# A decoder layer's embedding projection moved to the front of one core's weight stream

## The chip, the core and the metric

The kernel runs on one core of a Trainium2 chip. A time is the device time of one execution in microseconds (us); times of a kernel are the median of several executions. A profile is one further execution, recorded by the hardware profiler, with its own time. The engines of the core are TensorE (PE; its weight loads are PEld), VectorE (DVE), ScalarE (ACT), GpSimd (POOL) and SyncE (SP); each works through its own instructions in order, and data is moved by 16 DMA engines, which SP, POOL and ACT give transfers to.

## The reference, cut to what matters

One layer on x (512 x 2048, float32) and a per-layer embedding p (512 x 256):

```python
h = rms_norm(x, norm_g)
proj = h @ w_in                      # 2048 x 10800, split into q, k, v, gates, ...
o_a = nsa_attention(...) * silu(z_a)
o_b = spatial_gating(...) * silu(z_b)
merged = g_a * (o_a @ w_up_a) + g_b * (o_b @ w_up_b)
x = x + merged @ w_out
x = x + sigmoid(x @ w_ple_gate) * (p @ w_ple)      # w_ple: 256 x 2048
return rms_norm(x, final_g)
```

The change is about `p @ w_ple`. It needs only inputs; its result is wanted at the end, in the last gate.

## The kernel before, in words

**Arithmetic.** Every float32 operand is split in two: a high part rounded to the type `fp32r` (ACT, `high`, L96, instruction at L98 or L100) and the rest, the low part (DVE, `low`, L102, at L104 or L106). A product is three matmuls, high by high, high by low, low by high, added up in PSUM.

**The stream of jobs.** A `Job` is one product of an activation with a slice of a weight matrix. The jobs stand in one list (`add_job`, L121), and their weights come in this order through one queue: SP loads half a megabyte at a time into `raw`, three buffers (`load_to`, L134); ACT and DVE split it tile by tile into `hi` (four buffers) and `lo` (three) (`split_to`, L143); a load is issued when DVE has made the last low part of the load three places before it. `gemm` (L170) is a generator that issues the matmuls of the jobs; one step of it (`fill(1)`) is one unit of three 512-column matmuls. "T" jobs give a 128 x 512 tile in one PSUM bank (L190 to L192), "N" jobs four tiles of 128 x 512 or less in four banks (L198 to L200). At a job's end its `evac` function is issued. The rest of the kernel is written by hand around the stream: attention and the rest call `fill(n)` between their own instructions, so the order in which instructions stand in each engine's queue is that in which the program text issues them. `background` holds small pieces of work, of which `gemm` issues one or two (`pops`) for each weight tile.

**PSUM.** Eight banks, two for each of the tags g, s, t and o. `xs` is (g, g, s, s), `ys` is (t, t, o, o).

**The start (L548 to L608).** SP loads `g_row` (`norm_g`), the four 1 MB tiles of x and three weight loads. For each tile of 128 rows ACT sums squares (`stats`) and DVE scales (`scale`). TensorE transposes x in 16 pieces of four 128 x 128 blocks (`turn`), and ACT and DVE split each piece out of PSUM into `act_h` and `act_l` (`turned`). From the sixth piece on, two units of the first job, `kc0`, stand between them.

**Order of the jobs.** kc, vc, k, v, q and za (attention); vn, u, zb (gating); for each of 16 columns of tiles ma, mb, ua, ub (merge); then `pl0`, wo0 to wo3 (output projection), pg0, `pl1`, pg1, `pl2`, pg2, `pl3`, pg3 (the last gate). The four `pl` jobs (L456, L541) are p @ w_ple, 512 columns each, on `ys`; all wo and pg jobs have 16 steps of k, with wo on `xs` and `ys` in turn and pg on `xs`. p is loaded by POOL (L1010), transposed behind job ua8 and split into `ph` and `pl` (L1012 to L1016). `evac_ple` (L469) copies a pl job's banks to an SBUF tile `ple` on ACT, and `ple_add` (L477) multiplies it with the gate that ACT made in `evac_ple_gate` (L484) or `evac_last` (L503). At the end of wo3 the 64 KB a partition of `act_h` and `act_l` come free; the pool `fq` (L1027) then takes `fg` (`final_g`, loaded by POOL), `ple`, `th`, `tl` and `sg`.

Of the kernel before, what the change touches and what calls it, by code (L numbers as in the profile page):

```python
# [12 lines left out]
F32 = mybir.dt.float32  # L13
# [7 lines left out]
P = 128  # L21
S = 512
# [29 lines left out]
def kernel(ctx: ExitStack, tc: tile.TileContext, x, p, norm_g, w_in,  # L52
# [15 lines left out]
    def bank(kind, name):  # L68
        return psum.tile([P, 512], F32, tag=kind, name=name)
# [59 lines left out]
        jobs.append(job)  # L129

    raw, parts = {}, {}
    state = {"loads": 0, "high": 0, "low": 0, "ahead": 0, "pops": 2}

    def load_to(i):  # L134
        while state["loads"] <= min(i, len(loads) - 1):
# [34 lines left out]
    def gemm():  # L170
        si = 0
        for job in jobs:
# [4 lines left out]
            k = 0  # L177
            while k < job.kt - job.tail:
                flush()
                split_to(si + state["ahead"] + (k if job.tail else 0))  # L180
# [140 lines left out]
    def evac_c(which, a):  # L321
# [11 lines left out]
            deferred.append(rest)  # L333
        return f

    for a in range(2):
        add_job(Job(f"kc{a}", "T", w_in, C_KV + 128 * a, 128, KT, h_act, evac_c("k", a)))
    for a in range(2):
# [114 lines left out]
                nc.vector.tensor_tensor(out=sl, in0=sl, in1=ps[t], op=ALU.add)  # L453
        return e

    add_job(Job("pl0", "N", w_ple, 0, 512, 2, lambda k: p_act(k), lambda ps: evac_ple(0)(ps), ys))  # L456
    for cg in range(4):
        add_job(Job(f"wo{cg}", "N", w_out, 512 * cg, 512, KT, merged_act, evac_out(cg), (xs, ys)[cg % 2]))

# [2 lines left out]
            oa["l"][:, k] if k < 8 else ob_l[:, k - 8]  # L462

    f_tiles = {}

    def p_act(k):
        return f_tiles["ph"][:, k], f_tiles["pl"][:, k]

    def evac_ple(cg):  # L469
        def e(ps):  # L470
            t = f_tiles["pool"].tile([P, TT, 512], F32, tag="ple", name="ple")
            for i in range(TT):
                nc.scalar.copy(t[:, i], ps[i])
            f_tiles["ple"] = t
        return e
# [8 lines left out]
    def evac_ple_gate(cg):  # L484
        def e(ps):
            sg = [f_tiles["pool"].tile([P, 512], F32, tag="sg", name="sg", bufs=4) for _ in range(TT)]
            for t in range(TT):
                nc.scalar.activation(sg[t], ps[t], AF.Tanh, scale=0.5)
            ple = f_tiles["ple"]

            def add(t):
                ple_add(cg, t, sg[t], ple)

            def squares(t):
                sl = x2[:, t, 512 * cg:512 * cg + 512]
                nc.scalar.activation(sg[t], sl, AF.Square, accum_out=f_tiles["ss"][:, t, cg:cg + 1])
                nc.gpsimd.tensor_tensor(out=sl, in0=sl, in1=f_tiles["fg"][:, 512 * cg:512 * cg + 512], op=ALU.mult)
            for t in range(TT):
                background.append(lambda t=t: add(t))
                background.append(lambda t=t: squares(t))  # L500
        return e

    def evac_last(ps, t):  # L503
# [6 lines left out]
        if t:  # L510
# [4 lines left out]
        sl = ple_add(3, t, sg, f_tiles["ple"])  # L515
        nc.scalar.activation(sg, sl, AF.Square, accum_out=ss[:, t, 3:4])
        nc.vector.tensor_tensor(out=sl, in0=sl, in1=fg[:, 1536:], op=ALU.mult)
        if t == 0:
# [28 lines left out]

    with tc.tile_pool(name="xin", bufs=4, side="right") as xin:  # L548
        xt = [xin.tile([P, D], F32, tag="xt", name=f"xt{t}") for t in range(TT)]
        g_row = xin.tile([KT, P], F32, name="g_row", bufs=1)  # L550
        g_col = xin.tile([P, KT], F32, name="g_col", bufs=1)
        st = xin.tile([P, TT, 2], F32, name="st", bufs=1)
        nc.sync.dma_start(g_row, norm_g.rearrange("(k p) -> k p", p=P))
        for t in range(TT):
            nc.sync.dma_start(xt[t], x[t * P:t * P + P])
        load_to(2)

        def stats(t):
            sq = xin.tile([P, D], BF16, tag="sq", name="sq", bufs=1)
            nc.scalar.activation(sq, xt[t], AF.Square, accum_out=st[:, t, 0:1])  # L560
            nc.scalar.activation(st[:, t, 1:2], st[:, t, 0:1], AF.Sqrt, bias=eps_t, scale=1.0 / D)

        def scale(t):
            nc.vector.reciprocal(st[:, t, 0:1], st[:, t, 1:2])
            nc.vector.tensor_scalar(out=xt[t], in0=xt[t], scalar1=st[:, t, 0:1], scalar2=None, op0=ALU.mult)

        banks = {}

        def turn(hf, kp):

            b = banks[hf, kp] = bank("st"[len(banks) % 2], "ps_x")
            for j in range(4):
                k, t = 2 * kp + j // 2, 2 * hf + j % 2
                nc.tensor.transpose(b[:, j * P:j * P + P], xt[t][:, k * P:k * P + P], ident)

        def turned(hf, kp):
            sl = slice(2 * hf * P, 2 * hf * P + 2 * P)
            for j in range(2):
                k = 2 * kp + j
                split(act_h[:, k, sl], act_l[:, k, sl], banks[hf, kp][:, 2 * P * j:2 * P * (j + 1)],  # L580
                      g_col[:, k:k + 1], later=True)
            flush()

        b = bank("o", "ps_g")
        nc.tensor.transpose(b[:, :KT], g_row, ident[:KT, :KT])
        nc.vector.tensor_copy(g_col, b[:, :KT])
        for t in range(3):
            stats(t)
            if t < 2:
                scale(t)  # L590
        order = [(0, 0), (0, 1), (0, 2), (0, 3), (1, 0), (1, 1), (0, 4), (1, 2), (0, 5), (1, 3), (0, 6), (1, 4), (0, 7),
                 (1, 5), (1, 6), (1, 7)]
        for o in order[:4]:
            turn(*o)
        for i, o in enumerate(order):
            turned(*o)
            if i == 0:
                stats(3)
                scale(2)
                scale(3)  # L600
            if i + 4 < len(order):
                turn(*order[i + 4])
            if o[0] == 1 and o[1] >= 1:
                fill(2)
            elif o == (1, 0):
                split_to(0)
# [397 lines left out]
    f_tiles["ph"] = fp.tile([P, 2, S], F32R, name="ph")  # L1004
    f_tiles["pl"] = fp.tile([P, 2, S], F32R, name="pl")
    f_tiles["ss"] = fp.tile([P, TT, 4], F32, name="ss")
    with tc.tile_pool(name="sigp", bufs=2) as sigp:
        tmp_pool["p"] = sigp
        p_nat = sigp.tile([P, TT, 256], F32, name="p_nat", bufs=1)
        nc.gpsimd.dma_start(p_nat, p.rearrange("(t p) c -> p t c", p=P))  # L1010
        finish("ua8")
        for j in range(2):  # L1012
            b = bank("o", "ps_p")
            for t in range(TT):
                nc.tensor.transpose(b[:, t * P:t * P + P], p_nat[:, t, j * P:j * P + P], ident)
            split(f_tiles["ph"][:, j], f_tiles["pl"][:, j], b)  # L1016
        finish(f"ub{KT - 1}")
    ple0 = ctx.enter_context(tc.tile_pool(name="ple0", bufs=1))
    f_tiles["pool"] = ple0


    free_banks = {0: "gs", 1: "to", 2: "gs", 3: "to"}
    for cg in range(4):
        finish(f"wo{cg}")
        if cg == 3:
            ph_act.close()
            fq = f_tiles["pool"] = ctx.enter_context(tc.tile_pool(name="fq", bufs=2))  # L1027
            fg = f_tiles["fg"] = fq.tile([P, D], F32, name="fg", bufs=1)
            nc.gpsimd.dma_start(fg, bass.AP(tensor=final_g.tensor, offset=final_g.offset, ap=[[0, P], [1, D]]))
            f_tiles["th"] = fq.tile([P, 8, 512], F32R, name="th", bufs=1)  # L1030
            f_tiles["tl"] = fq.tile([P, 8, 512], F32R, name="tl", bufs=1)
            state["pops"] = 1
# [38 lines left out]
```

## Time and profile before

| | |
|---|---|
| time, median of 3 runs | 1666.81 us (1666.53 to 1667.07) |
| the profiled execution's own time | 1666.61 us |
| its span, first to last instruction | 1664.9 us |
| mean granted clock of TensorE | 0.997 |
| busy: PE, PEld, DVE, ACT, POOL | 98%, 82%, 44%, 37%, 6% |
| matmuls and transposes | 7821 |
| DMA | 159.62 MB, mean 96 GB/s |

In the lines of the profile, L12 is line 12 of the kernel; `out<-in` are the program's names for the tiles; a row of a timeline has the start, the duration, engine, line, operation, tiles, shapes and count, and in brackets how long the engine stood idle before it and what released it. Matmuls are pipelined: a 512-column matmul is shown with 0.39 us, while the next one starts sooner than that. In the chain of waits stands the work that ended last, followed back from the last instruction.

### The profile page before, as it was taken

The page shows a single profiled execution, that of the slowest core. Times are in us where ns is not written, and L with a number is a line of the kernel's source. Part 1 is how long each engine was busy: PE and PEld are TensorE (multiplying, and loading weights), DVE is VectorE, ACT ScalarE, POOL GpSimd, SP SyncE. Part 2 cuts the span into 40 slices and gives each one's busy share as a digit, 9 for nine tenths or more (in the row PEclk, how much of TensorE's full clock was granted, in tenths as well). Part 3 has the DMA queues.
Part 4 walks back from the last instruction along what each step waited for, and adds up shares of the span by engine and source line. Part 5 has one row for each costly group of instructions (what it writes and reads, how often), then busy time and mean ns, then how long its engine had stood idle before and what let it go on. Part 6 is the DMA issues. An engine that isn't in the chain of part 4 may idle for free.

```text
span 1664.9 us, 20578 instructions
## 1 busy us (share of the span) xinstructions
PE 1638.9 (98%) x7821; PEld 1367.3 (82%) x7821; DVE 739.0 (44%) x1492; ACT 619.1 (37%) x1255; POOL 107.8 (6%) x136
## 2 busy tenths in 40 slices
PE   6999999999999999999999999999999999999997
PEld 5779888888888888888888888888888888888886
DVE  5343478888873352443223222322235333333335
ACT  6233366676653322332222222222224222223334
POOL 2000010110210011000000000000000000001100
PEclk9999999999999999999999999999999999999999
DMA  6322421111133333334333333333334422333333
GB/s 201 93 76 76 112 64 39 52 51 51 45 113 109 89 89 92 99 90 113 102 96 94 101 94 97 99 91 101 99 92 159 140 93 89 91 125 89 101 101 127
DMA packets 214625, 159.62 MB, mean 96 GB/s; under 512 B 4848, under 2 KB 190336, under 8 KB 212992
## 3 DMA queue, kind: packets, MB, share of 16 engines
q1 hardware_dynamic: 212976, 151.05, 31.3%
q0 software_dynamic: 1408, 6.92, 1.2%
q8 instruction: 61, 1.00, 0.2%
q14 instruction: 36, 0.29, 0.1%
q10 hardware_dynamic: 144, 0.36, 0.1%
HBM read 154.12 MB, written 4.19 MB: 95 GB/s over the span
## 4 chain that ended last, share of the span: by engine, by line
PE 95%; DVE 3%; ACT 1%; DMA 0%; issue 0%; SPq 0%; DVEq 0%; ACTq 0%
PE ps_wo L200 4%; PE ps_wo L198 4%; PE ps_wo L199 3%; PE ps_mb L190 3%; PE ps_ma L190 3%; PE ps_mb L191 3%; PE ps_ma L191 3%; PE ps_ma L192 3%; PE ps_mb L192 3%; PE ps_pg L198 3%; PE ps_pg L200 3%; PE ps_pg L199 3%; PE ps_za L190 2%; PE ps_za L192 2%; PE ps_t L768 2%; PE ps_za L191 2%
## 5 line engine op out<-in xcount | busy, mean ns | idle before, releaser
L104 DVE TENSOR_TENSOR lo<-raw,hi 128x512 fp32r<-128x512 f32 (+1 forms) x536 | 367.4, 688 | 652.9 <-PE ps_mb L192 129.7
L98 ACT CAST hi<-raw 128x512 fp32r<-128x512 f32 (+1 forms) x536 | 328.6, 615 | 730.9 <-PE ps_wo L200 102.5
L198 PE MATMUL ps_wo<-hi,act_h 128*128 128x512 f32 x256 | 100.9, 394 | 0.0
L200 PE MATMUL ps_wo<-hi,act_l 128*128 128x512 f32 x256 | 99.8, 390 | 0.0
L199 PE MATMUL ps_wo<-lo,act_h 128*128 128x512 f32 x256 | 99.7, 390 | 0.0
L190 PE MATMUL ps_ma<-act_h,hi 128*128 128x512 f32 x256 | 99.6, 389 | 0.0
L191 PE MATMUL ps_ma<-act_l,hi 128*128 128x512 f32 x256 | 99.6, 389 | 0.0
L192 PE MATMUL ps_ma<-act_h,lo 128*128 128x512 f32 x256 | 99.6, 389 | 0.0
L190 PE MATMUL ps_mb<-act_h,hi 128*128 128x512 f32 x256 | 99.6, 389 | 0.0
L191 PE MATMUL ps_mb<-act_l,hi 128*128 128x512 f32 x256 | 99.6, 389 | 0.0
L192 PE MATMUL ps_mb<-act_h,lo 128*128 128x512 f32 x256 | 99.6, 389 | 0.0
L98 ACT CAST pth<-ps_t 128x512 fp32r<-128x512 f32 (+1 forms) x88 | 47.9, 544 | 65.7 <-PE ps_t L768 65.4
L729 ACT ACTIVATE prob<-prob,st 128x512 f32<-128x512 f32 (+3 forms) x128 | 70.7, 555 | 4.0 <-DVE st L720 3.8
L104 DVE TENSOR_TENSOR ptl<-ps_t,pth 128x512 fp32r<-128x512 f32 (+1 forms) x88 | 56.3, 640 | 21.1 <-ACT pth L98 20.3
L720 DVE CUSTOM_DVE_ANT_0 prob<-ps_s,b 128x512 f32<-128x512 f32 (+3 forms) x128 | 56.3, 486 | 10.1 <-PE ps_s L717 9.8
L431 POOL TENSOR_TENSOR m<-sig,sig 128x512 f32<-128x512 f32 x16 | 27.1, 1694 | 493.6 <-DVE sig L429 493.6
L200 PEld LDWEIGHTS ps_wo<-hi,act_l 128*128 128x128 f32 x256 | 48.1, 188 | 10.2
L192 PEld LDWEIGHTS ps_mb<-act_h,lo 128*128 128x128 f32 x256 | 48.1, 188 | 10.0
L192 PEld LDWEIGHTS ps_ma<-act_h,lo 128*128 128x128 f32 x256 | 48.1, 188 | 10.0
L190 PEld LDWEIGHTS ps_ma<-act_h,hi 128*128 128x128 f32 x256 | 48.1, 188 | 10.0
L190 PEld LDWEIGHTS ps_mb<-act_h,hi 128*128 128x128 f32 x256 | 48.1, 188 | 10.0
L191 PEld LDWEIGHTS ps_ma<-act_l,hi 128*128 128x128 f32 x256 | 48.1, 188 | 9.9
(311 smaller groups left out, 3663.8 us busy)
## 6 DMA issues: line engine op xcount, KB each, us to landing
raw<-in_w_in_dram SPq DMA_DIRECT2D x164, 512.0 KB, 3.5
raw<-in_w_out_dram SPq DMA_DIRECT2D x32, 512.0 KB, 3.5
raw<-in_w_ple_gate_dram SPq DMA_DIRECT2D x32, 512.0 KB, 3.5
raw<-in_w_up_a_dram SPq DMA_DIRECT2D x16, 512.0 KB, 3.7
raw<-in_w_up_b_dram SPq DMA_DIRECT2D x16, 512.0 KB, 3.7
xt<-in_x_dram SPq DMA_DIRECT2D x4, 1024.0 KB, 8.0
m<-in_x_dram POOLq DMA_DIRECT2D x4, 1024.0 KB, 8.6
out_dram<-m SPq DMA_DIRECT2D x3, 1024.0 KB, 3.9
```

What stands on the lines that cost most here:

```text
L98: nc.scalar.copy(hi, src)
L104: nc.vector.tensor_tensor(out=lo, in0=src, in1=hi.bitcast(F32), op=ALU.subtract)
L190: nc.tensor.matmul(ps, hi[:, j], ah, start=st, stop=False)
L191: nc.tensor.matmul(ps, hi[:, j], al, start=False, stop=False)
L192: nc.tensor.matmul(ps, lo[:, j], ah, start=False, stop=sp)
L198: nc.tensor.matmul(o, ah[:, sl], hi[:, j], start=st, stop=False)
L199: nc.tensor.matmul(o, ah[:, sl], lo[:, j], start=False, stop=False)
L200: nc.tensor.matmul(o, al[:, sl], hi[:, j], start=False, stop=sp)
L431: nc.gpsimd.tensor_tensor(out=merge_tiles["m"][:, f], in0=merge_tiles[0], in1=t, op=ALU.add)
L720: nc.vector.tensor_tensor_reduce(out=pt[:, j * n:j * n + n], in0=o[:, j], in1=b0[:, 512 - n:], scale=-SLOPE[h], scalar=3.0e38, op0=ALU.add ...
L729: nc.scalar.activation(sl, sl, AF.Exp, bias=st[:, 0, j, hh:hh + 1], scale=-1.0, accum_out=st[:, 1, j, hh:hh + 1])
L768: nc.tensor.transpose(b[:, (2 * e + hh) * P:(2 * e + hh + 1) * P], pts[hh][:, c:c + P], ident)
```

## The change

The four `pl` jobs become the first four jobs of the stream. Their results leave PSUM on DVE and ACT (`d` and `a` in the string) into half-job tiles of 512 KB, three buffers, and POOL stores these in a scratch tensor `spill` in device memory, 4 MB in all. At the end of wo3 POOL loads the four tiles back into four `ple` buffers of `fq`, and the gates use those. The late transposes of p and the pl jobs between the pg jobs are gone.

At the start, p and two weight loads now go ahead of x on SP's queue, and a weight load ahead of each of the last two tiles of x; `g_row` goes to POOL. Ten small matmuls of the identity are issued to TensorE first (`keep_busy`). x is scaled tile by tile between the pl jobs: the squares of x0 and x1 stand behind pl0 in the queues, those of x2 behind pl1, those of x3 behind pl2. Three units of pl3 follow, and then x is transposed in 16 pieces of another cut: a piece is one of the 16 k-tiles with all four row tiles. The last five units of pl3 and fourteen of kc0 stand between the pieces. p's split tiles and the squares' output lie in `ob_h` and `ob_l`, which are unused then.

```diff
-    def split_to(i):
-        while state["high"] <= min(i + 1, len(subs) - 1):
+    def split_to(i, more=1):
+        while state["high"] <= min(i + more, len(subs) - 1):
...
+    pl_in, ple_t = {}, {}
+    dram = ctx.enter_context(tc.tile_pool(name="dram", bufs=1, space=bass.MemoryType.DRAM))
+    spill = dram.tile([S, D], F32, name="spill")
+
+    def evac_ple(cg):
+        def f(ps):
+            for a in range(0, TT, 2):
+                o = pl_in["pool"].tile([P, 2, 512], F32, tag="ple", name="ple", bufs=3)
+                for t in (a, a + 1):
+                    if "dddd aadd ddaa adad".split()[cg][t] == "a":
+                        nc.scalar.copy(o[:, t - a], ps[t])
+                    else:
+                        nc.vector.tensor_copy(o[:, t - a], ps[t])
+                nc.gpsimd.dma_start(spilled(cg)[:, a:a + 2], o)
+        return f
+
+    def spilled(cg):
+        return spill[:, 512 * cg:512 * cg + 512].rearrange("(t p) c -> p t c", p=P)
+
+    for cg in range(4):
+        add_job(Job(f"pl{cg}", "N", w_ple, 512 * cg, 512, 2, lambda k: (pl_in["h"][:, k], pl_in["l"][:, k]),
+                    evac_ple(cg), (xs, ys)[cg % 2]))
...
-    add_job(Job("pl0", "N", w_ple, 0, 512, 2, lambda k: p_act(k), lambda ps: evac_ple(0)(ps), ys))
...
-        if cg:
-            add_job(Job(f"pl{cg}", "N", w_ple, 512 * cg, 512, 2, p_act, evac_ple(cg), ys))
...
+        pl_in["h"], pl_in["l"] = ob_h[:, 0:2], ob_l[:, 0:2]
+        sq = ob_h[:, 4:8].rearrange("p f t -> p (f t)")
...
-        nc.sync.dma_start(g_row, norm_g.rearrange("(k p) -> k p", p=P))
+        nc.sync.dma_start(p_nat, p.rearrange("(t p) c -> p t c", p=P))
+        nc.gpsimd.dma_start(g_row, norm_g.rearrange("(k p) -> k p", p=P))
+        load_to(1)
         for t in range(TT):
+            if t > 1:
+                load_to(t)
             nc.sync.dma_start(xt[t], x[t * P:t * P + P])
-        load_to(2)
+        spin = bank("o", "ps_spin")
+
+        def keep_busy(n):
+
+            for _ in range(n):
+                nc.tensor.matmul(spin[:, :P], ident, ident, start=True, stop=True)
...
+        def turn(k):
+            b = banks[k] = bank("ssgssstotosstoto"[k], "ps_x")
+            for t in range(TT):
+                nc.tensor.transpose(b[:, t * P:t * P + P], xt[t][:, k * P:k * P + P], ident)
+
+        def turned(k):
+            split(act_h[:, k], act_l[:, k], banks[k], g_col[:, k:k + 1])
+
+        keep_busy(10)
+        state["more"] = 0
+        for j in range(2):
+            b = bank("t", "ps_p")
+            for t in range(TT):
+                nc.tensor.transpose(b[:, t * P:t * P + P], p_nat[:, t, j * P:j * P + P], ident)
+            split(pl_in["h"][:, j], pl_in["l"][:, j], b)
+            split_to(j, 0)
         b = bank("o", "ps_g")
         nc.tensor.transpose(b[:, :KT], g_row, ident[:KT, :KT])
+        split_to(3, 0)
+        fill(8)
         nc.vector.tensor_copy(g_col, b[:, :KT])
-        for t in range(3):
+        for t in range(2):
             stats(t)
...
+            scale(t)
+        split_to(5, 0)
+        fill(8)
+        stats(2)
+        scale(2)
+        split_to(7, 0)
+        fill(8)
+        stats(3)
+        scale(3)
+        split_to(8, 0)
+        fill(3)
+        turn(0)
+        turn(1)
+        turned(0)
+        fill(1)
+        turn(2)
+        turned(1)
+        fill(2)
+        turn(3)
+        turned(2)
+        fill(2)
+        for k in range(4, KT):
+            turn(k)
+            turned(k - 1)
+            if k % 4 == 0:
+                split_to(8 + k // 4, 0)
+            fill(1)
+        turned(KT - 1)
+        state["more"] = 1
         state["ahead"] = 2
-        split_to(5)
+        fill(2)
+        split_to(13)
...
-        p_nat = sigp.tile([P, TT, 256], F32, name="p_nat", bufs=1)
-        nc.gpsimd.dma_start(p_nat, p.rearrange("(t p) c -> p t c", p=P))
-        finish("ua8")
-        for j in range(2):
-            b = bank("o", "ps_p")
-            for t in range(TT):
-                nc.tensor.transpose(b[:, t * P:t * P + P], p_nat[:, t, j * P:j * P + P], ident)
-            split(f_tiles["ph"][:, j], f_tiles["pl"][:, j], b)
...
+            for i in range(4):
+                ple_t[i] = fq.tile([P, TT, 512], F32, tag="ple", name="ple", bufs=4)
+                nc.gpsimd.dma_start(ple_t[i], spilled(i))
```

More of the change, by code (lines that the diff above doesn't have):

```diff
@@ L131 @@
     raw, parts = {}, {}
-    state = {"loads": 0, "high": 0, "low": 0, "ahead": 0, "pops": 2}
+    state = {"loads": 0, "high": 0, "low": 0, "ahead": 0, "more": 1, "pops": 2}
     def load_to(i):
@@ L179, in gemm @@
                 flush()
-                split_to(si + state["ahead"] + (k if job.tail else 0))
+                split_to(si + state["ahead"] + (k if job.tail else 0), state["more"])
                 for _ in range(state["pops"]):
@@ L464 @@
     f_tiles = {}
[L466 to L475, printed above, removed]
     def ple_add(cg, t, sg, ple):
@@ L488, in e @@
                 nc.scalar.activation(sg[t], ps[t], AF.Tanh, scale=0.5)
-            ple = f_tiles["ple"]
             def add(t):
-                ple_add(cg, t, sg[t], ple)
+                ple_add(cg, t, sg[t], ple_t[cg])
             def squares(t):
@@ L514, in evac_last @@
                                 op0=ALU.mult, op1=ALU.add)
-        sl = ple_add(3, t, sg, f_tiles["ple"])
+        sl = ple_add(3, t, sg, ple_t[3])
         nc.scalar.activation(sg, sl, AF.Square, accum_out=ss[:, t, 3:4])
@@ L549 @@
         xt = [xin.tile([P, D], F32, tag="xt", name=f"xt{t}") for t in range(TT)]
+        pl_in["pool"] = xin
+        p_nat = xin.tile([P, TT, 256], F32, name="p_nat", bufs=1)
+        pl_in["h"], pl_in["l"] = ob_h[:, 0:2], ob_l[:, 0:2]
+        sq = ob_h[:, 4:8].rearrange("p f t -> p (f t)")
         g_row = xin.tile([KT, P], F32, name="g_row", bufs=1)
@@ L552 @@
         st = xin.tile([P, TT, 2], F32, name="st", bufs=1)
-        nc.sync.dma_start(g_row, norm_g.rearrange("(k p) -> k p", p=P))
+        nc.sync.dma_start(p_nat, p.rearrange("(t p) c -> p t c", p=P))
+        nc.gpsimd.dma_start(g_row, norm_g.rearrange("(k p) -> k p", p=P))
+        load_to(1)
         for t in range(TT):
+            if t > 1:
+                load_to(t)
             nc.sync.dma_start(xt[t], x[t * P:t * P + P])
-        load_to(2)
+        spin = bank("o", "ps_spin")
+        def keep_busy(n):
+            for _ in range(n):
+                nc.tensor.matmul(spin[:, :P], ident, ident, start=True, stop=True)
         def stats(t):
-            sq = xin.tile([P, D], BF16, tag="sq", name="sq", bufs=1)
             nc.scalar.activation(sq, xt[t], AF.Square, accum_out=st[:, t, 0:1])
@@ L567 @@
         banks = {}
[L569 to L577, printed above, removed]
-            for j in range(2):
[L579 to L582, printed above, removed]
+        def turn(k):
+            b = banks[k] = bank("ssgssstotosstoto"[k], "ps_x")
+            for t in range(TT):
+                nc.tensor.transpose(b[:, t * P:t * P + P], xt[t][:, k * P:k * P + P], ident)
@@ L586 @@
+        fill(8)
         nc.vector.tensor_copy(g_col, b[:, :KT])
-        for t in range(3):
+        for t in range(2):
             stats(t)
[L589 to L606, printed above, removed]
+            scale(t)
@@ L1003 @@
     fp = ctx.enter_context(tc.tile_pool(name="fp", bufs=1))
-    f_tiles["ph"] = fp.tile([P, 2, S], F32R, name="ph")
-    f_tiles["pl"] = fp.tile([P, 2, S], F32R, name="pl")
     f_tiles["ss"] = fp.tile([P, TT, 4], F32, name="ss")
@@ L1008 @@
         tmp_pool["p"] = sigp
-        p_nat = sigp.tile([P, TT, 256], F32, name="p_nat", bufs=1)
-        nc.gpsimd.dma_start(p_nat, p.rearrange("(t p) c -> p t c", p=P))
-        finish("ua8")
-        for j in range(2):
-            b = bank("o", "ps_p")
-            for t in range(TT):
-                nc.tensor.transpose(b[:, t * P:t * P + P], p_nat[:, t, j * P:j * P + P], ident)
-            split(f_tiles["ph"][:, j], f_tiles["pl"][:, j], b)
         finish(f"ub{KT - 1}")
-    ple0 = ctx.enter_context(tc.tile_pool(name="ple0", bufs=1))
-    f_tiles["pool"] = ple0
     free_banks = {0: "gs", 1: "to", 2: "gs", 3: "to"}
```

## The prediction, as put on record before the change was run

> **What bounds the kernel now.** I read the page, then the chain of waits in order of time, then TensorE's timeline of the first 36 us with the clock by window.
>
> ```profile
> span 1664.9 us, 20578 instructions
> ...
> PE 95%; DVE 3%; ACT 1%; DMA 0%; issue 0%; SPq 0%; DVEq 0%; ACTq 0%
> ```
>
> The chain is TensorE for 95% of the span. A change that removes no matmul can gain only where it isn't, and one such place is the start (chain of waits: start, us, what):
>
> ```profile
> 1.72 7.00 DMA xt<-in_x_dram
> ...
> 12.65 0.92 PE ps_x L574 x3
> ...
> 73.01 1.04 PE ps_hid L654 x8
> ...
> 1042.37 0.87 PE ps_p L1015 x8
> ```
>
> For 12.65 us the chain loads, squares and scales x. TensorE in that time and up to unit 15 of the first job (a unit is what one `fill` step issues: three 512-column matmuls):
>
> ```profile
> 10.15 0.47 PE L574 MATMUL ps_x<-ident,xt 128*128 128x128 f32 x1 [7.44 <-DVE xt L565]
> 12.65 3.46 PE L574 MATMUL ps_x<-ident,xt 128*128 128x128 f32 x15 [2.02 <-DVE xt L565]
> 16.87 0.31 PE L574 MATMUL ps_x<-ident,xt 128*128 128x128 f32 x1 [0.77 <-DVE st L564]
> 18.22 0.55 PE L574 MATMUL ps_x<-ident,xt 128*128 128x128 f32 x3 [1.03 <-DVE xt L565]
> 19.09 0.63 PE L574 MATMUL ps_x<-ident,xt 128*128 128x128 f32 x4 [0.33 <-DVE act_l L106]
> 19.87 2.79 PE L574 MATMUL ps_x<-ident,xt 128*128 128x128 f32 x12 [0.16 <-DVE act_l L106]
> ...
> 23.35 0.48 PE L190 MATMUL ps_kc<-act_h,hi 128*128 128x512 f32 x1
> ...
> 27.07 1.03 PE L574 MATMUL ps_x<-ident,xt 128*128 128x128 f32 x8
> ...
> 29.32 1.03 PE L574 MATMUL ps_x<-ident,xt 128*128 128x128 f32 x8
> ...
> 35.67 0.39 PE L190 MATMUL ps_kc<-act_h,hi 128*128 128x512 f32 x1
> ```
>
> The first product starts at 23.35 and unit 15 of kc0 at 35.67. Whatever the changed kernel does in front, it is judged by when that unit starts there. One period of 8 transposes and 6 matmuls is 29.32 - 27.07 = 2.25 us. The granted clock by window (columns: stretch, its length, PE, PEld, DVE, ACT, POOL busy, clock, DMA share, GB/s):
>
> ```profile
> 18.00:20.00 2.00, 1.30 (x8) 0.89 (x9) 2.00 (x6) 2.00 (x6) 0.00 (x0) 0.93 0.00 0
> 20.00:22.00 2.00, 2.00 (x10) 1.93 (x11) 2.00 (x6) 2.00 (x7) 0.00 (x0) 0.50 0.00 0
> 22.00:24.00 2.00, 1.84 (x11) 1.38 (x10) 2.00 (x6) 1.96 (x6) 0.00 (x0) 0.72 0.00 0
> 24.00:26.00 2.00, 2.00 (x15) 1.75 (x14) 2.00 (x6) 1.53 (x5) 0.00 (x0) 1.00 0.00 0
> ```
>
> At 0.50 the twelve transposes of 19.87 take 2.79 / 12 = 0.23 us each; at 1.00 eight take 1.03. The fifteen of 12.65 also take 0.23, so I read the start as half clock, although no drop is recorded there. The half clock begins near 19.7, after a stretch (16.1 on) with gaps of 0.77, 1.03 and 0.33 us, and lasts until about 23.
>
> **What it removes.** The four embedding jobs leave their places. The first of them, on TensorE's timeline:
>
> ```profile
> 1277.03 0.39 PE L198 MATMUL ps_pl<-hi,ph 128*128 128x512 f32 x1
> ...
> 1282.47 0.39 PE L198 MATMUL ps_wo<-hi,act_h 128*128 128x512 f32 x1
> ```
>
> A job is 24 matmuls in 5.44 us (0.227 each), all on the path: 4 x 5.44 = 21.76. The eight transposes of p at 1042.37 add 0.87. **Removed: 22.63 us.**
>
> **What it adds in front.** Loads (us to landing last), then durations from the timeline:
>
> ```profile
> m<-in_x_dram POOLq DMA_DIRECT2D x4, 1024.0 KB, 8.6
> ...
> raw<-in_w_ple_dram SPq DMA_DIRECT2D x4, 512.0 KB, 3.5
> ...
> w1v<-in_cmp_w_v_dram POOLq DMA_DIRECT2D x1, 512.0 KB, 7.4
> ...
> p_nat<-in_p_dram POOLq DMA_DIRECT2D x1, 512.0 KB, 4.3
> ```
>
> ```profile
> 0.81 0.39 SPq L553 DMA_DIRECT2D g_row<-in_norm_g_dram  x1
> 1.08 0.29 POOL masks.py:199 TENSOR_SCALAR_AFFINE_SELECT ident<-ident 128x128 f32<-128x128 f32 x1
> ...
> 6.24 1.91 ACT L560 ACTIVATE sq<-xt 128x2048 bf16<-128x2048 f32 x1 [3.94 <-DMA xt<-in_x_dram]
> ...
> 8.74 1.91 ACT L560 ACTIVATE sq<-xt 128x2048 bf16<-128x2048 f32 x1 [0.17 <-DMA xt<-in_x_dram]
> 8.80 1.29 DVE L565 TENSOR_SCALAR xt<-xt,st 128x2048 f32<-128x2048 f32 x1
> ...
> 1042.85 1.07 ACT L98 CAST ph<-ps_p 128x512 fp32r<-128x512 f32 x2 [2.76 <-PE ps_p L1015]
> ...
> 1043.46 1.29 DVE L104 TENSOR_TENSOR pl<-ps_p,ph 128x512 fp32r<-128x512 f32 x2 [0.30 <-ACT ph L98]
> ```
>
> - *Start.* p_nat is now SP's first load: 0.8 + 3.5 = 4.3. Between 6.24 and 8.74 a megabyte of x landed, 2.5 us, so each half megabyte behind it costs 1.25: the first two weights land at 5.6 and 6.8, x0 at 9.3, x1 at 11.8, the third weight at 13.1, x2 at 15.6. The fourth weight load needs the first's buffer, so SP waits there for DVE's low half of the second weight tile (8.4, below), with x3 and all later weights behind it; the data already queued runs until 15.6, so this costs nothing, and x3 lands near 19.4. `g_row`, 8 KB, moves to POOL's queue; it is wanted before pl0, at 7.
> - *Splits.* Four transposes of p at half clock end at 5.3; then come ACT's cast of p, its cast of the weight and DVE's two subtractions, each 0.6 behind the other: pl0 starts at 7.0. The ten warm-up matmuls run from 1.4 (`ident`) beside the load and, if each takes the 0.23 of a transpose, end at 3.7: nothing.
> - *Three jobs.* 3 x 5.44 = 16.3. If the clock becomes full 0 to 3.4 us into pl0, this adds 0 to 1.7; I take 0.85: pl2 ends at 24.2. DVE stays ahead: after pl0 it has a last copy and `g_col`, two scalings and a subtraction (0.9 + 2 x 1.5 + 0.7 = 4.6 us), and pl2's first product comes 5.44 us after pl0.
> - *The wait that then decides.* ACT runs in order, so the squares of x3 stand behind ACT's copy of pl2's last bank: 0.7, and then what the rows take from 6.24 to 8.80 + 1.29 = 10.09, 3.85. x3 is scaled at 24.2 + 0.7 + 3.85 = 28.8. TensorE meanwhile has three units of pl3 (to 26.3), the transposes of x0 to x2 of the first turn, then nothing: some 2.3 us idle.
> - *The rest.* At full clock: five transposes 0.6, the five other units of pl3 3.4, turns 2 and 3 0.9, twelve loop steps at 2.25 / 2 = 1.13 make 13.5, two units 1.4: 19.8. DVE needs 0.65 per turned tile and 0.17 for weights a step, under 1.13. Turn 5's bank waits for a subtraction queued behind pl3's copies, 0.4. Unit 15 would start at 28.8 + 19.8 + 0.4 = 49.0, which is **13.3 later** than 35.67.
>
> **The clock after the idle.** 2.1 us of gaps in the 3.5 us before 19.7 were followed by 3.3 us at half clock. An idle of 2.3 us should do the same where at least 1.9 of it falls into one such stretch, which by the share of phases (2.0 of 3.4) is 6 in 10. It costs half of 3.4: 0 or 1.7. I take **1.7**. The Trainium skill, "TensorE: Matmul & The Clock Gate", section "HAM oscillation — how this bites in real kernels", asks for an idle gap above some 3.4 us before the clock falls. By that rule this term would be 0 and the forecast 1.7 lower. The trace differs: its longest gap before the fall was 1.03 us.
>
> **The spill.** 16 copies and eight 512 KB stores. Rows for this and the next part (forms of `ple`; then ACT, DVE and TensorE timelines):
>
> ```profile
> L473 ACT COPY ple<-ps_pl x16: 564/587/607, 1281.9 to 1611.6; 128x512 f32<-128x512 f32 x16
> ```
>
> ```profile
> 1277.23 0.69 DVE L429 SCALAR_TENSOR_TENSOR sig<-sig,ps_ub 128x512 f32<-128x512 f32 x1 [0.46 <-PE ps_ub L192]
> ...
> 1292.46 0.62 ACT L98 CAST hi<-raw 128x512 fp32r<-128x512 f32 x1 [3.68 <-DMA raw<-in_w_out_dram]
> ...
> 1506.17 2.64 ACT L488 ACTIVATE sg<-ps_pg 128x512 f32<-128x512 f32 x4
> ...
> 1508.01 0.39 PE L198 MATMUL ps_pl<-hi,ph 128*128 128x512 f32 x1
> ```
>
> A copy is 0.6 and lies beside the next job. There are three buffers, so the fourth and sixth half-job wait for the first and third store, which have about 5.5 us to land; POOL's half-megabyte loads took 4.3 to 7.4. A store from POOL is not shown: bounds 0 and 2.0 us, since ACT's squares of x3 stand behind the sixth. I take 0.5, nearer to the 4.3. POOL waits for each copy, and behind stand the index tiles and the compression weights, wanted at 73.01: nothing.
>
> **Later places.** wo0 now follows ub15 directly; its second bank is freed by DVE at 1277.23 + 0.69 = 1277.92 and wanted at 1277.03 + 0.68: **0.25**. Each pg job follows the one before on the same banks. ACT frees the first at 1506.17 + 0.66 = 1506.83, before 1508.01, and the others 0.66 apart against 0.68: nothing. The four 1 MB reloads queue on POOL behind `final_g` at the end of wo3, 5 MB or 12 us of data, beside the weights. The nearest row is x's second load (4 MB, 8.6 us to landing), when ACT waited 3.68 us for a weight; the wait list has none of TensorE for it. I take 0, bounds 0 and 3. POOL's next products come after 1506 and meet nothing. ACT's old copies leave the late stage, where matmuls hid them: no gain.
>
> **Sum:** -22.63 + 13.3 + 1.7 + 0.5 + 0.25 = -6.9 us. The profiled run took 1666.61 (span 1664.9), 0.2 under the median of 1666.81; from that, 1666.8 - 6.9 = **1659.9**.
>
> **Rivals.**
> 1. *Half clock through the front jobs.* If the short waits for loads and splits keep the clock at 0.50, the 72 matmuls of pl0 to pl2 cost 0.227 more each, 16.3, less the 0.85 counted: 1675.4, slower. It decides from 6.9 / 0.227 = 30 such matmuls. For it: the start is at half clock now. Against: the products from 23.35 are at full clock after 3.4 us of transposes. 0.10. The Trainium skill, same page, section "Part 4: PE-mode transpose", says that transposes don't raise the clock. The trace differs: only transposes ran from 19.87 to 23, when it rose.
> 2. *The gain is eaten by waits in queues:* stores that hold ACT 2.0, half clock in pl0 for its full 1.7, reloads that hold TensorE 3: 1.5 + 0.85 + 3 more, 1665.3. For it: 7.4 and 3.68 above; against: TensorE's slack there. 0.10.
> 3. *Everything early:* full clock from pl0 on, no fall after the idle, stores in time, 0.85 + 1.7 + 0.5 less: 1656.9; without the idle too, 1654.5. 0.15.
> 4. *It does not do what it says:* the front jobs only push x back, and unit 15 comes 22 us later: 1666.8, no change. Against: TensorE has nothing before 10.15. 0.05.
>
> The forecast, 1657 to 1663, has 0.60. The range of **1655.5 to 1666.0** leaves out rivals 1 and 4 and a third of 3. A measurement here tells 0.2%, 3.3 us, from no change. Forecast, rival 3 and half of 2 are faster, 0.80; the rest of 2 and most of 4 the same, 0.09; slower 0.11.
>
> **What would show it.** Right: unit 15 of kc0 at 49 to 51; pl0's first product near 7; an idle of 2 to 3 us before x3's first transpose, with ACT's squares right behind its copy of pl2; 0.50 in the clock's rows after that; no gap between pg jobs. Wrong: a matmul spacing of 0.45 in pl1 (rival 1), ACT's or DVE's copies waiting for a store, TensorE waiting for a weight near 1460 (rival 2), or no idle at all (rival 3).

## The result and the profile after

The changed kernel takes **1662.24 us** (median of 8 runs, 1660.22 to 1662.99), beside 1666.87 us for the kernel before (8 runs, 1666.53 to 1667.29): a ratio of **0.997**, 95% interval 0.9959 to 0.9981. It is faster by 4.6 us; 6.9 were forecast. The profiled execution is one of the longer ones: 1662.88 us, 3.7 under that of before. From the page after:

```profile
span 1661.2 us, 20583 instructions
...
PE 96%; DVE 2%; ACT 1%; DMA 0%; issue 0%; POOL 0%; DVEq 0%; POOLq 0%; ACTq 0%
...
spill<-ple POOLq DMA_DIRECT2D x8, 512.0 KB, 5.6
```

TensorE is on the chain for 96% of the span, where it was 95%. What still isn't TensorE is told by the chain in order of time (start, us, what):

```profile
19.13 7.11 DMA spill<-ple
26.32 1.08 ACT ple L346 x2
27.40 1.91 ACT ob_h L579 x2
29.85 1.30 DVE xt L584
31.20 1.33 PE ps_x L591 x5
```

In before the chain began with x's load. Here a *store* stands on it: a half-job of p @ w_ple that POOL began to write out at 19.13 and that landed 7.11 us later. ACT's copy waits for it, and behind the copy come the squares of x3, its scaling, its transposes. The same stretch on TensorE:

```profile
1.43 4.64 PE L576 MATMUL ps_spin<-ident 128*128 128x128 f32 x20 [1.43 <-POOL eps_t L74]
5.86 1.22 PE L601 MATMUL ps_p<-ident,p_nat 128*128 128x128 f32 x8
...
7.84 0.50 PE L198 MATMUL ps_pl<-hi,ob_h 128*128 128x512 f32 x1 [0.59 <-ACT hi L98]
8.64 0.50 PE L199 MATMUL ps_pl<-lo,ob_h 128*128 128x512 f32 x1 [0.30 <-DVE lo L104]
8.98 0.39 PE L200 MATMUL ps_pl<-hi,ob_l 128*128 128x512 f32 x1
9.21 0.39 PE L198 MATMUL ps_pl<-hi,ob_h 128*128 128x512 f32 x1
...
24.84 0.39 PE L198 MATMUL ps_pl<-hi,ob_h 128*128 128x512 f32 x1
...
27.51 0.49 PE L591 MATMUL ps_x<-ident,xt 128*128 128x128 f32 x3
31.20 1.33 PE L591 MATMUL ps_x<-ident,xt 128*128 128x128 f32 x5 [3.20 <-DVE xt L584]
...
54.45 0.40 PE L190 MATMUL ps_kc<-act_h,hi 128*128 128x512 f32 x1
```

pl0 starts at 7.84 with matmuls 0.23 apart, pl3 at 24.84. Then TensorE turns what it can of x and idles 3.20 us for x3. Unit 15 of kc0 starts at 54.45, which is 18.8 later than in before; the prediction's terms (13.3 + 1.7 + 0.5) gave 15.5. The windows (the columns are those named in the prediction) show what the idle did to the clock:

```profile
28.00:30.00 2.00, 0.00 (x0) 0.00 (x0) 0.31 (x2) 1.97 (x4) 1.05 (x2) 1.00 1.08 295
30.00:32.00 2.00, 0.80 (x4) 0.81 (x5) 1.74 (x2) 0.42 (x2) 0.00 (x0) 0.53 1.05 422
32.00:34.00 2.00, 2.00 (x8) 1.60 (x7) 1.46 (x2) 1.09 (x2) 0.00 (x0) 0.50 0.22 88
34.00:36.00 2.00, 2.00 (x8) 1.71 (x7) 0.62 (x2) 0.71 (x2) 0.00 (x0) 0.50 0.00 0
36.00:38.00 2.00, 2.00 (x10) 1.54 (x10) 0.86 (x2) 0.56 (x1) 0.00 (x0) 0.76 0.00 0
```

The clock falls to 0.50 while TensorE idles and comes back near 36.95, so TensorE works 36.95 - 31.20 = 5.75 us at half speed, which costs half of that, 2.9 us. The DMA share is above 1 from 28 to 32 in these rows, and near 1 from 2 us up to then: the stores share the DMA engines with the loads of x and of the weights. Who waits for the stores, and since when each was on its way (timelines of POOL, DVE and ACT):

```profile
13.81 0.76 POOL L349 DMA_DIRECT2D spill<-ple  x1 [11.57 <-DVE ple L348]
...
19.13 0.73 POOL L349 DMA_DIRECT2D spill<-ple  x1 [2.66 <-ACT ple L346]
...
22.22 1.29 DVE L348 COPY ple<-ps_pl 128x512 f32<-128x512 f32 x2 [3.29 <-DMA spill<-ple]
...
26.32 1.08 ACT L346 COPY ple<-ps_pl 128x512 f32<-128x512 f32 x2 [4.23 <-DMA spill<-ple]
27.28 1.93 ACT L579 ACTIVATE ob_h<-xt 128x2048 fp32r<-128x2048 f32 x1
```

The first store, issued at 13.81, releases DVE at 22.22, 8.4 us later; the third, issued at 19.13, releases ACT at 26.32. The 5.6 of the profile's page is the median over all eight; the last two, issued at 38.43 and 40.25 when the loads ahead of them are done, landed in 3.1 and 4.1.

Late in the kernel (the end of ub15 and the start of wo0 on TensorE, then what DVE does there):

```profile
1294.97 0.39 PE L198 MATMUL ps_wo<-hi,act_h 128*128 128x512 f32 x1
...
1295.91 0.50 PE L198 MATMUL ps_wo<-hi,act_h 128*128 128x512 f32 x1
...
1296.72 0.39 PE L198 MATMUL ps_wo<-hi,act_h 128*128 128x512 f32 x1
```

```profile
1295.17 0.69 DVE L451 SCALAR_TENSOR_TENSOR sig<-sig,ps_ub 128x512 f32<-128x512 f32 x1 [0.47 <-PE ps_ub L192]
```

The second product is due at 1294.97 + 0.68 = 1295.65 and starts at 1295.91, when DVE has read its bank; the third is 0.81 behind it, where 0.68 is usual: 0.4 in all. Between the pg jobs there is no gap, and the four reloads (13.1 us to landing) make no matmul wait. The bookkeeping closes: 18.8 + 0.4 - 22.63 = -3.4, and the last matmul starts at 1651.46 where it started at 1654.89. The other 0.3 of the 3.7 lie behind it.

### The profile page after: what moved, and what is told of

The parts are those of the page before. It is cut to its first block, busy times and chain, and to the rows that moved or that the text cites. A ratio compares the mean times of both kernels' runs of the same rounds, so it can differ in the third digit from the quotient of the medians.

```text
span 1661.2 us, 20583 instructions
## 1 busy us (share of the span) xinstructions
PE 1643.5 (99%) x7841; PEld 1370.3 (82%) x7841; DVE 743.5 (45%) x1486; ACT 612.6 (37%) x1229; POOL 116.9 (7%) x148
## 4 chain that ended last, share of the span: by engine, by line
PE 96%; DVE 2%; ACT 1%; DMA 0%; issue 0%; POOL 0%; DVEq 0%; POOLq 0%; ACTq 0%
PE ps_wo L198 4%; PE ps_ma L190 3%; PE ps_mb L190 3%; PE ps_wo L199 3%; PE ps_mb L191 3%; PE ps_ma L192 3%; PE ps_ma L191 3%; PE ps_wo L200 3%; PE ps_mb L192 3%; PE ps_pg L198 3%; PE ps_pg L200 3%; PE ps_pg L199 3%; PE ps_t L802 2%; PE ps_za L190 2%; PE ps_za L192 2%; PE ps_za L191 2%
## 5 line engine op out<-in xcount | busy, mean ns | idle before, releaser
L200 PEld LDWEIGHTS ps_wo<-hi,act_l 128*128 128x128 f32 x256 | 48.1, 188 | 10.3
L198 PEld LDWEIGHTS ps_wo<-hi,act_h 128*128 128x128 f32 x256 | 48.1, 188 | 10.2 <-DVE sig L451 0.5
```

The costliest lines, as they stand in the source:

```text
L198: nc.tensor.matmul(o, ah[:, sl], hi[:, j], start=st, stop=False)
L200: nc.tensor.matmul(o, al[:, sl], hi[:, j], start=False, stop=sp)
```

## The experiments

**Theory:** the stores' landing holds ACT's copy (and DVE's), x3's squares stand behind that copy, and the idle that follows makes the clock fall; these three links are the 2.3 us that are missing (1662.24 against the forecast 1659.9). **Rivals:** x3's place behind pl2 alone makes the delay, with the stores in slack; or the clock alone does, by chance of its phase; or the start is spoilt by the warm-up. All times are medians of the runs of that kernel; the ratios are to the kernel before as it ran beside them: 1666.87 us beside the change, 1666.63 (9 runs) beside the kernels without stores, with four buffers, with matmuls in the idle and with x3 before pl2, and 1666.71 (17 runs) beside the other four. The last four columns are from each profiled execution; "idle" is TensorE's wait for the scaling of x3.

| kernel | us (lowest to highest) | ratio to before, 95% | x3's squares start | idle | unit 15 |
|---|---|---|---|---|---|
| the change | 1662.24 (1660.22 to 1662.99) | 0.9959 to 0.9981 | 27.28 | 3.20 | 54.45 |
| without stores | 1660.16 (1660.06 to 1660.45) | 0.9948 to 0.9973 | 25.63 | 2.05 | 51.71 |
| four buffers | 1659.71 (1658.80 to 1660.47) | 0.9943 to 0.9970 | 25.59 | 2.26 | 51.72 |
| two buffers | 1666.36 (1665.11 to 1666.81) | 0.9988 to 1.0006 | 31.55 | 3.69 | 58.40 |
| matmuls in the idle | 1660.27 (1660.21 to 1660.62) | 0.9949 to 0.9974 | 27.61 | 0.49 | 52.09 |
| x3 before pl2 | 1657.49 (1657.02 to 1657.85) | 0.9931 to 0.9956 | 22.13 | none | 49.33 |
| x3 before pl2, four buffers | 1656.45 (1656.26 to 1656.79) | 0.9925 to 0.9952 | 22.29 | none | 48.01 |
| the same, short warm-up | 1656.83 (1656.16 to 1657.04) | 0.9927 to 0.9952 | 22.53 | none | 48.02 |
| one warm-up matmul | 1661.92 (1661.23 to 1662.70) | 0.9961 to 0.9982 | 26.96 | 2.47 | 53.05 |

**Without stores.** The half-jobs are copied out of PSUM but not written to `spill`; the last stage loads pieces of x in their place, so that traffic stays as it was.

```diff
-                nc.gpsimd.dma_start(spilled(cg)[:, a:a + 2], o)
...
-                nc.gpsimd.dma_start(ple_t[i], spilled(i))
+                nc.gpsimd.dma_start(ple_t[i], x[:, 512 * i:512 * i + 512].rearrange("(t p) c -> p t c", p=P))
```

> Leaves out the eight stores of p @ w_ple, and reloads 4 MB of x in their place, so the product in the last gate is not that of the layer. Theory (stores): ACT and DVE no longer wait for a store; ACT's squares of x3 start near 25.5 us instead of 27.28, x3 is scaled at 29.4 instead of 31.14, TensorE's idle is 2.0 us instead of 3.2, and unit 15 of kc0 starts at 49.6 if the clock stays full and up to 52.5 if it falls for two windows, instead of 54.45: 1658.0 to 1660.9 us. Rival (TensorE's own work and ACT's order set when x3 is scaled, the stores only fill time that was free): unit 15 stays at 53.5 or later and the time within 1 us of 1662.2.

ACT's copy of pl2's last banks now waits for TensorE alone, and the squares follow at once (timeline of ACT, then of TensorE):

```profile
24.47 1.27 ACT L346 COPY ple<-ps_pl 128x512 f32<-128x512 f32 x2 [2.27 <-PE ps_pl L200]
...
29.54 0.77 PE L590 MATMUL ps_x<-ident,xt 128*128 128x128 f32 x5 [2.05 <-DVE xt L583]
```

x3's squares start 1.65 us earlier, and unit 15 2.7 earlier: the clock is at 0.50 for one stretch (30.3 to 33.7) in place of two:

```profile
30.00:32.00 2.00, 2.00 (x11) 1.63 (x9) 1.46 (x3) 1.17 (x2) 0.00 (x0) 0.58 0.00 0
32.00:34.00 2.00, 2.00 (x7) 1.62 (x6) 0.78 (x2) 1.06 (x2) 0.00 (x0) 0.57 0.00 0
```

So the stores hold x3 back, directly, by some 1.7 us. That they do it by the landing and not by DMA traffic is shown by the next kernel.

**Four buffers for the half-jobs.** The stores stay; p's own tile becomes the fourth buffer, since no space is left.

```diff
-                o = pl_in["pool"].tile([P, 2, 512], F32, tag="ple", name="ple", bufs=3)
+                o = pl_in["pool"].tile([P, 2, 512], F32, tag="ple", name="ple", bufs=4)
...
-        p_nat = xin.tile([P, TT, 256], F32, name="p_nat", bufs=1)
+        p_nat = xin.tile([P, TT, 256], F32, tag="ple", name="p_nat", bufs=4)
```

> A fourth staging buffer in front of the stores (p's own tile, free after its transposes). Theory (stores): the fourth half-job waits for nothing and the sixth for the second store, issued at 15.2 us, instead of the third, issued at 19.1; the copies of pl2 on ACT start by 24.5, x3 is scaled near 29.5, unit 15 at 50 to 52.6: 1658.3 to 1661 us, as without stores within 0.5. Rival (the stores also cost by what they take from the loads of x): x3 lands too late for ACT, and half or more of what leaving the stores out gains is missing here.

```profile
24.63 1.08 ACT L346 COPY ple<-ps_pl 128x512 f32<-128x512 f32 x2 [2.67 <-DMA spill<-ple]
...
29.50 1.19 PE L591 MATMUL ps_x<-ident,xt 128*128 128x128 f32 x5 [2.26 <-DVE xt L584]
```

The copy still waits for a store, but for the second, and only up to 24.63, the time at which it starts without stores too (24.47). Idle and unit 15 are nearly those of the kernel without stores, and the time is no higher (1659.71 beside 1660.16). All eight stores are still written, so it is the wait for the buffer that counts, and not what the stores take from other transfers.

**Two buffers**, one fewer than in the change: a larger dose.

```diff
-                o = pl_in["pool"].tile([P, 2, 512], F32, tag="ple", name="ple", bufs=3)
+                o = pl_in["pool"].tile([P, 2, 512], F32, tag="ple", name="ple", bufs=2)
```

> Two buffers for the half-jobs in place of three, nothing else: the third copy now waits for the first store, the fourth for the second, and so on, a larger dose of the suspected wait. Theory (stores that land 7 to 8 us after their issue hold ACT's copies, and x3's squares stand behind these): x3 is scaled 3 to 6 us later than 31.1, TensorE's idle before it grows from 3.2 to 6 to 9 us, unit 15 of kc0 at 57 to 61, time 1665.5 to 1669. Rival (the copies' waits are slack, and x3's place in the order is all that matters): unit 15 at 54.5, time 1662.2 as with three.

```profile
22.80 1.07 ACT L346 COPY ple<-ps_pl 128x512 f32<-128x512 f32 x2 [6.18 <-DMA spill<-ple]
...
30.60 1.07 ACT L346 COPY ple<-ps_pl 128x512 f32<-128x512 f32 x2 [3.47 <-DMA spill<-ple]
```

The squares of x3 start 4.3 us later than in the change, unit 15 3.95 later, and the time is 4.1 higher. The theory's 6 to 9 us of idle are there, but not all in one place: 3.69 us stand before x3 and 3.5 more in three waits ahead of it (1.56, 1.51 and 0.44), where pl3's weights and first turn wait behind the same copies. The whole gain of the change is gone, with a ratio of 0.9997 (0.9988 to 1.0006). The rival with the stores in slack expected no difference and falls.

**Matmuls in the idle.** Fourteen more products of the identity stand before the first turn of x, on a bank that is free then. Nothing starts earlier; TensorE only isn't idle.

```diff
         split_to(8, 0)
         fill(3)
+        spin = bank("g", "ps_spin2")
+        keep_busy(14)
         turn(0)
```

> 14 more matmuls of the identity (28 passes of 0.11, some 3.1 us) issued to TensorE in its idle before x3's first transpose. Theory (clock): the idle is what brings the clock to 0.50 for two windows; filled, the clock's row stays at 1.00, x3 is scaled no earlier (31.1), but unit 15 starts 2.9 us earlier, at 51.5: 1659.9 us in the profiled run, and the spread of the runs of one kernel (2.8 us now) falls below 1. Rival (the fall of the clock has another cause than the idle): 0.50 stands there as before and the time within 0.5 of 1662.2.

Two of the windows shown above:

```profile
30.00:32.00 2.00, 1.50 (x14) 1.27 (x13) 1.97 (x3) 0.57 (x2) 0.00 (x0) 1.00 1.05 420
32.00:34.00 2.00, 2.00 (x14) 1.69 (x13) 1.46 (x3) 1.71 (x3) 0.00 (x0) 1.00 0.24 96
```

ACT's copy still waits for its store and x3's squares start 0.3 later than in the change, but the clock stays at 1.00, and unit 15 comes 2.4 earlier. The time falls by 2.0 us against the change, and its scatter from 2.8 us to 0.4. So the clock's fall is a cost by itself. That it alone makes the missing 2.3 us does not fit the kernels without stores and with four buffers, which gain as much (2.1 and 2.5) although the clock still falls in their profiled runs.

The fall isn't the same in every run of one kernel. The eight runs of the change lie in three groups: 1660.2 and 1660.4, 1661.6 and 1661.7, and four from 1662.8 to 1663.0, with a mean granted clock of 0.999, 0.998 and 0.996. The first group takes the time of the kernel with the idle filled. I read the three as no, one and two stretches at 0.50; only the last has a profile. So the median holds some chance.

**x3 before pl2.** The squares and the scaling of x3 are issued one job earlier, ahead of the copies that wait for stores.

```diff
         split_to(7, 0)
-        fill(8)
         stats(3)
         scale(3)
+        fill(8)
         split_to(8, 0)
```

> The squares and the scaling of x3 are issued ahead of pl2 instead of behind it. Theory (order of ACT's queue): the squares start when x3 lands, near 22.6, DVE scales x3 behind its weights' low parts at 26.1 to 27.4, and TensorE goes from pl3's third unit into the transposes with less than 0.5 us idle; the clock stays at 1.00; unit 15 at 48.5: 1656.8 us. Rival (x3 arrives too late or DVE is the bound, since DVE still waits for the first store at 22.2): an idle of 2 us or more stays, with the clock's fall, unit 15 at 52 or later: 1660 or more.

Timelines of ACT and TensorE:

```profile
22.13 1.92 ACT L579 ACTIVATE ob_h<-xt 128x2048 fp32r<-128x2048 f32 x1 [0.16 <-DMA xt<-in_x_dram]
...
33.31 0.59 ACT L346 COPY ple<-ps_pl 128x512 f32<-128x512 f32 x1 [2.15 <-DMA spill<-ple]
...
35.42 0.63 PE L591 MATMUL ps_x<-ident,xt 128*128 128x128 f32 x4 [1.21 <-DVE act_l L106]
```

This takes away the idle and the fall of the clock together: 4.75 us less than the change. The squares now start when x3 lands. What is late next is again a copy behind a store, of pl3 this time: it holds the splitting of x's pieces, and TensorE waits 1.21. For that the kernel is 0.8 later at unit 15 and 0.7 us slower than its theory said (48.5, 1656.8).

**x3 before pl2 and four buffers**, the two edits above in one kernel.

> x3's squares and scaling ahead of pl2 in the queues, and four buffers for the half-jobs. Theory (the landing of the stores holds the copies, the place of x3 behind pl2 makes the idle, the two are separate links of one chain): with x3 early, TensorE still waits 1.2 us at 35.4, for ACT's and DVE's copies of pl3 that stand behind a store; four buffers take most of it away. No idle before x3, no fall of the clock, unit 15 of kc0 at 48.0 to 48.7 (49.33 with x3 early alone), time 1656.2 to 1657.0. Rival (with x3 early the stores are off the path and the 1.2 us is something else, DVE's queue for instance): the wait stays, unit 15 at 49.3, time 1657.5 as with x3 early alone.

```profile
34.09 0.63 PE L591 MATMUL ps_x<-ident,xt 128*128 128x128 f32 x4 [0.39 <-DVE act_l L106]
```

This is the only idle time that TensorE's timeline shows between 20 and 60 us. Time and unit 15 are where the theory put them; the rival's (1657.5, 49.3) are not. It is the fastest version: **1656.45 us**, ratio 0.9939 (0.9925 to 0.9952), 10.3 us under the kernel before, more than twice the gain of the change.

**One warm-up matmul** in place of ten, on the change as it is.

```diff
-        keep_busy(10)
+        keep_busy(1)
```

> One warm-up matmul (two passes) in place of ten (twenty passes). The ten end at 6.07, and p has landed at 4.9, so they hold p's transposes back by about 1 us. Theory (the warm-up is paid back: p's transposes and pl0 run at full clock because of it): without it p's transposes start at 4.9, take 0.23 each, pl0 starts about 0.3 earlier, but its matmuls run at 0.45 for 3.4 us or so, which costs 1.7 less what began earlier: unit 15 of kc0 0.5 to 1.5 later than 54.45, time 1662.7 to 1664. Rival (pl0 would be at full clock anyway, the warm-up only delays): pl0 at 0.227 a matmul, 0.5 to 1 us earlier, time 1661.3 to 1661.8. The fall of the clock before x3 lies behind this and has its own scatter of some 2.8 us, so the place of pl0's end is to be read, not the time alone.

```profile
4.87 1.97 PE L601 MATMUL ps_p<-ident,p_nat 128*128 128x128 f32 x8 [2.65 <-DMA p_nat<-in_p_dram]
...
7.18 0.79 PE L198 MATMUL ps_pl<-hi,ob_h 128*128 128x512 f32 x1
...
9.43 0.63 PE L199 MATMUL ps_pl<-lo,ob_h 128*128 128x512 f32 x1
9.86 0.63 PE L200 MATMUL ps_pl<-hi,ob_l 128*128 128x512 f32 x1
...
14.77 0.39 PE L198 MATMUL ps_pl<-hi,ob_h 128*128 128x512 f32 x1
```

```profile
26.00 1.08 ACT L346 COPY ple<-ps_pl 128x512 f32<-128x512 f32 x2 [3.11 <-DMA spill<-ple]
```

pl0 starts 0.66 earlier and runs 0.43 a matmul up to 11.12 (then 0.23), so pl1 starts at 14.77, where it started at 13.96: the warm-up does what its theory says, and pays 0.8 us there. Yet the time is no higher (1661.92, with intervals that all but coincide): the 0.8 goes into the wait for the store, which here ends at 26.00. (Unit 15 is earlier than in the change because this profiled run has one stretch at 0.50, from 31.6 to 35.0, and not two.) The theory's time (1662.7 to 1664) missed, and so did the rival's mechanism, a pl0 at full clock.

**Short warm-up**: the fastest version with seven warm-up matmuls in place of ten.

```diff
-        keep_busy(10)
+        keep_busy(7)
```

> As the kernel with x3 early and four buffers, with seven warm-up matmuls (fourteen passes, 3.2 us) in place of ten (4.6). Theory (the warm-up ends at 4.7, when p lands at 4.9, and the clock is full by then or soon after): p's transposes start near 4.9 in place of 5.86, pl0 0.6 to 0.9 us earlier, time 0.5 to 0.9 us under that kernel, 1655.5 to 1656. Rival (the clock needs the longer run before p): p's transposes and the first matmuls at half clock, pl0 ends no earlier or up to 1 us later, time the same to 1 us over.

Timelines of TensorE, then of ACT:

```profile
1.43 3.36 PE L576 MATMUL ps_spin<-ident 128*128 128x128 f32 x14 [1.43 <-POOL eps_t L74]
4.88 1.96 PE L601 MATMUL ps_p<-ident,p_nat 128*128 128x128 f32 x8
...
7.18 0.49 PE L198 MATMUL ps_pl<-hi,ob_h 128*128 128x512 f32 x1 [0.18 <-ACT hi L98]
```

```profile
22.53 1.92 ACT L579 ACTIVATE ob_h<-xt 128x2048 fp32r<-128x2048 f32 x1 [1.06 <-DMA xt<-in_x_dram]
...
28.43 0.62 ACT L98 CAST hi<-raw 128x512 fp32r<-128x512 f32 x1 [2.60 <-DMA raw<-in_w_in_dram]
```

p's transposes are at half clock, as the rival has it. pl0 starts 0.9 earlier than in the fastest version and at full clock, as the theory has it, but nothing is left of it at unit 15 (48.02 beside 48.01). The time is the same within its scatter, where the theory had 1655.5 to 1656. ACT now waits 1.06 for x3 and 2.60 for a weight, and gets that weight at 28.43; with ten warm-up matmuls it got it at 28.32. With the DMA share near 1 from 4 to 32 us in both, I take it that the front is bound by its bytes now; that was not tested by itself.

## Why the prediction was right, and where its sum was not

The direction, the place of the loss and its chain were right; the term for the stores was too small, that for the clock too small in the profiled run, and the front came late.

Of the prediction's own signs of being right, three came (x3's squares right behind ACT's copy, 0.50 in the clock's rows, no gap between pg jobs) and three did not: unit 15 at 54.45 where it said 49 to 51, pl0 at 7.84 where it said near 7, an idle of 3.20 where it said 2 to 3. One of its signs of being wrong came too: copies that wait for a store. So the time lies within the forecast's 1657 to 1663, but near its upper end, and the width of that range has a part in it.

- *Removed:* -22.63, as forecast: the late jobs and transposes are gone, with no gap between the pg jobs.
- *Start and splits:* p lands at 4.9 where 4.3 was forecast. The ten warm-up matmuls, costed at nothing, stand in the trace as twenty (to 6.07) and delay p's transposes. pl0 starts at 7.84, not 7.0. In return it runs at full clock, so the 0.85 for a cold clock isn't spent. pl2 ends at 24.84, 0.65 later than forecast. With one warm-up matmul pl0 ended 0.8 later still, and the wait for the store hid it. x3 landed near 22.1 and not near 19.4 (its squares wait for it until 22.13 where they stand ahead of pl2); in the change ACT isn't free by then, so this cost nothing.
- *The wait that then decides:* right. From the end of ACT's copy (27.28) the forecast's 3.85 lead to 31.13; x3 is scaled at 31.14.
- *The spill,* the term that was mis-sized most: "I take 0.5" of bounds 0 and 2.0. Two kernels give 1.7 (27.28 against 25.59 and 25.63). The forecast had the right buffers and stores, but gave these 5.5 us to land, and they took 8.3 and 7.1. It leaned on 4.3, the landing of p's load in the middle of the kernel, although its rows showed 7.4 too, and although it had x's tiles landing up to 19.4. The Trainium skill, "DMA: Bandwidth & Descriptors", section "Anatomy of one DMA — SWDGE (gpsimd) path", fits such a transfer with 2.0 us and its bytes at 436 GB/s. That is an estimate of 3.2 us for 512 KB. The trace agrees where there is little other traffic (3.1 for the store issued at 38.43, with a DMA share of 0.14 from 38 to 40); beside a share of 1 the two landings that count took more than twice that.
- *The clock:* 1.7 forecast. In the profiled run two stretches at 0.50 cost 2.9; over the runs, the kernel with matmuls in the idle puts it at 2.0 (1662.24 - 1660.27). The idle was 3.20, where 2.3 was forecast. By the windows the clock fell at 30.1, when TensorE had been idle for 2.1 us and was still idle, and was down for 6.8 us; with two buffers it fell at 33.8, again 2.1 us into the idle, and was down for 6.7. With idles of 2.05, 2.26 and 2.47 (no stores, four buffers, one warm-up matmul) it fell when TensorE was at work again, and was down for 3.4. That the idle left after the fall brings the second stretch is argued from these five, not shown.
- *The rest:* 20.2 forecast; from 31.20 to 54.45 are 23.25, less 2.9 makes 20.35. Right.
- *Later places:* wo0's wait 0.26, beside the forecast's 0.25 (its rows give 1277.92 - 1277.71 = 0.21), and 0.13 for the start after it. The reloads cost nothing.

So unit 15 of the profiled run is off by 0.65 (front) + 1.2 (spill) + 1.2 (clock) + 0.15 (the rest) = 3.2: 54.45 beside the 51.2 of 49.0 + 1.7 + 0.5. For the median, with 2.0 for the clock, it is 0.65 + 1.2 + 0.3 + 0.15 = 2.3, which is what 1662.24 lies above 1659.9: the theory's three links are 1.5 of it, and the rest is the late front and a small remainder.

**Rival 1** (half clock in the front jobs) did not come, thanks to the warm-up; a part of it, in pl0, is seen when that is cut to one matmul. **Rival 2** is half true: its 2.0 for stores is nearly what was measured, its reloads and its half clock are not. **Rival 3** (no fall of the clock, stores in time, no idle; 1656.9 to 1654.5) is what the kernel with x3 before pl2 and four buffers reaches, 1656.45: the prediction's list of what stands in the way was the list of what to mend. **Rival 4** (22 us later, no change in time) falls by the time, whose ratio's interval ends at 0.9981; the 18.8 alone would not tell, since it is as far from 22 as from 15.5.

On the clock, the rule that the prediction cited (the Trainium skill, "TensorE: Matmul & The Clock Gate", "HAM oscillation — how this bites in real kernels": idle above some 3.4 us) does not hold in these runs either: the clock fell after idles of 2.05, 2.26 and 2.47 us and 2.1 us into those of 3.20 and 3.69. It stayed up after 0.49 and 1.21, and, with two buffers, after 1.56 and 1.51 with 0.50 us of work between them.

## What to carry to other kernels

When work is moved into the front of a stream, look at what is *queued behind* its evacuation: here a store's landing, through a buffer too few, stood on the chain of the whole kernel, and moving one line was worth as much as the change itself. Cost a transfer by rows taken where the DMA engines are as busy as they will be then, not by its median. And a short idle of TensorE may have to be paid twice, as the idle and as the half clock after it; matmuls of no use in the idle told the two apart.

## What the runs showed of the hardware

- Ten float32 products of 128 x 128 stand in the trace as twenty matmuls of 0.23 us each (1.43 to 6.07), while a float32 transpose of the same size stands there as one. In the filled idle, at a clock of 1.00, 28 such matmuls take 3.29 us, 0.12 each.
- With seven warm-up matmuls TensorE is busy from 1.43 on, p's transposes at 4.88 still take 0.24 each (1.96 / 8), and pl0's products from 7.18 on are at full speed. The recorded clock is 1.00 in all of that time, also where products are 0.43 apart (9.43 and 9.86 with one warm-up matmul): at the start the spacing tells the clock, and the record doesn't.
- The clock's fall can widen a kernel's scatter: the runs of the change lie within 2.8 us, and with the idle filled within 0.4. An open idle needn't: without stores, where the profiled clock falls after 2.05 us, the runs lie within 0.4 too.
